# Attention scores on one core: waits folded into TensorE's matmuls, and one signal per tile from SyncE

## The chip, the cores and the metric

The kernel runs on one core of a Trainium2 chip. The metric is device microseconds of one execution, as the median of several runs; lower is better.

## The reference

```python
def setup_inputs():
    batch, heads, seq, dim = 8, 8, 512, 64
    # q, k: [8, 8, 512, 64] float32, normal

def reference(q, k):
    scale = 1.0 / np.sqrt(q.shape[-1])
    return (np.einsum('bhqd,bhkd->bhqk', q, k) * scale).astype(np.float32)
```

For each of 64 pairs of batch and head the 512 queries are multiplied with the 512 keys over a depth of 64, and scaled by 1/8. The inputs are 2 x 8.4 MB, the output is 67.1 MB of float32.

## The kernel before

**Tiles.** The batch is cut into four units (UNITS) of two batch entries. A unit's k and q are loaded in two DMAs of 2 MB into one of three buffers `big`, cast to bf16 by GpSimd into `xb`, turned by TensorE (`turn`, eight transposes with an identity into the PSUM tile `tp`) and moved by ScalarE and VectorE (`move`) into `kT` (keys) and `qz` (queries, with zeros so that two heads share one matmul of depth 128). A unit gives four output tiles of 4 MB (CHUNKS), so there are 16 tiles g = 0 to 15. A tile is one store DMA from a buffer `big`; the three buffers rotate, so tile g uses the buffer of tile g-3, and those of the loads before that.

**One tile.** `scores` makes eight pairs p = 0 to 7 of two matmuls (128 x 512 each) into the PSUM tiles `ps` p mod 3. The even pairs are scaled and copied to `big` by ScalarE, the odd ones by VectorE (`evacuator`, 128 x 1024 elements at once). Between pairs 2 and 3, as long as there is a later unit to prepare (g < 12), TensorE turns one chunk of it out of `xs`, which GpSimd has filled from `xb` (`fill`), and ScalarE and VectorE move it after their pairs 1 and 2.

**Order.** Nothing is scheduled by a planner: each engine has its own program, and semaphores order them. TensorE's tiles are a hardware loop (`pe.Fori`), so its semaphores are counted down again each time; `take` (L161) waits for a count and subtracts it in one instruction of TensorE's sequencer. The semaphores around the change are:

- `next`: tile g+1 may begin. SyncE raises it at L97, when ScalarE (`out_act`) and VectorE (`out_dve`) are done with their halves of tile g, and then issues the store of tile g (L98).
- `room`: the store buffer of the tile is free. For the first three tiles GpSimd raises it after the casts that read the buffer (L143); for the others it waits at L152 for the landing of store g-2 (`store_sems`) and raises it. TensorE takes it between the two matmuls of pair 0 (L171).
- `free0`, `free1`, `free2`: a PSUM tile is empty. Raised by the evacuation (L234), taken ahead of pairs 2 to 7.
- `ready`: `xs` is filled. `moved`: the turned chunk is in place. `turn`: a chunk is turned. `pe_act`, `pe_dve`: a pair is computed. `cast`: the buffer of the second unit has been read, so that the last unit can be loaded into it.

GpSimd does in one loop (L148) the fill for tile g's successor and then the wait for a landed store. SyncE's queue holds, in order, the six first loads, the two loads of the last unit (each behind `cast`), and the sixteen stores; at its end it waits for the last landings.

Of the kernel before, what the change touches and what calls it, by code (L numbers as in the profile page):

```python
# [5 lines left out]
def kernel(  # L6
# [5 lines left out]
    nc = tc.nc  # L12
# [3 lines left out]
    UNITS = B // 2  # L16
# [11 lines left out]
    CHUNKS = 4  # L28
    SLOTS = 12
    PAIRS = RO  # L30
# [4 lines left out]


    names = ["ready", "room", "moved", "zeroed", "ident", "turn", "pe_act", "pe_dve",
             "next", "free0", "free1", "free2", "out_act", "out_dve", "cast"]
    sem = {name: nc.alloc_semaphore(name) for name in names}
    load_sems = [nc.alloc_semaphore(f"load{n}") for n in range(2 * UNITS)]  # L40
    store_sems = [nc.alloc_semaphore(f"store{n}") for n in range(3)]
# [9 lines left out]
    qz = nc.alloc_sbuf_tensor("qz", [P, 2 * N, RO, P], bf16)[:]  # L51
    identity = nc.alloc_sbuf_tensor("identity", [P, P], f32)[:]
    tp = nc.alloc_psum_tensor("tp", [P, W, P], f32)[:]
    pss = [nc.alloc_psum_tensor(f"ps{n}", [P, 2, S], f32)[:] for n in range(3)]

    def words(ap):
        return ap.bitcast(f32)
# [7 lines left out]
    xsw = words(xs.rearrange("p w s d e -> p w (s d e)"))  # L65
    keys = kT.rearrange("p n m s j -> p n (m s j)")

    pe = nc.tensor
# [3 lines left out]
    def xf(v):  # L72
        return bigs[(0, 1, 2, 1)[v]].rearrange("p x i k -> p (x i k)").rearrange(
            "p (x s c) -> p x s c", x=2, s=2)

    def store_buffer(g):
        return bigs[(0, 2, 1)[g % 3]]

    def load(v, x):
        nc.sync.dma_start(out=xf(v)[:, x],  # L80
                          in_=(k_r, q_r)[x][v].rearrange("p (s c) -> p s c", s=2)
                          ).then_inc(load_sems[2 * v + x], 16)
# [6 lines left out]
    tc.compile()  # L89


    for x in range(2):
        nc.sync.wait_ge(sem["cast"], x + 1)
        load(UNITS - 1, x)
    for g in range(CHUNKS * UNITS):
        nc.sync.wait_ge(sem["out_act"], g + 1)
        nc.sync.wait_ge(sem["out_dve"], g + 1).then_inc(sem["next"], 1)  # L97
        nc.sync.dma_start(out=out_r[g], in_=store_buffer(g).rearrange("p x i k -> p x (i k)")  # L98
                          ).then_inc(store_sems[g % 3], 16)
    for n in range(3):  # L100
        nc.sync.wait_ge(store_sems[n], 16 * len(range(n, 4 * UNITS, 3)))

# [4 lines left out]
                            fill=1.0, base=0, pattern=[[-1, P]], channel_multiplier=1  # L107
                            ).then_inc(sem["ident"], 1)

    def fill(copy, c):  # L110
        w0 = c % SLOTS * W
        copy(out=xs.rearrange("p w s d e -> p (w s d e)"),  # L112
             in_=xb[:, w0:w0 + W].rearrange("p w s d e -> p (w s d e)")).then_inc(sem["ready"], 1)
# [11 lines left out]
    for v in range(UNITS):  # L125
        for x in range(2):
# [18 lines left out]
                nc.gpsimd.drain().then_inc(sem["cast"], 1)  # L145
            elif v == 1 and x == 1:
                last.then_inc(sem["cast"], 1)
    for g in range(2, CHUNKS * UNITS - 1):  # L148
        if g + CHUNKS < CHUNKS * UNITS:
            nc.gpsimd.wait_ge(sem["turn"], g + CHUNKS)  # L150
            fill(nc.gpsimd.tensor_copy, g + CHUNKS)
        nc.gpsimd.wait_ge(store_sems[(g - 2) % 3], 16 * ((g - 2) // 3 + 1)  # L152
                          ).then_inc(sem["room"], 1)


    def turn(src, dst):
        for w in range(W):
            ins = pe.transpose(out=dst[:, w], identity=identity, in_=src[:, w])  # L158
        ins.then_inc(sem["turn"], 1)

    def take(name, count=1):  # L161
        pe.wait_ge(sem[name], count).then_inc(sem[name], -count)  # L162


    def scores(n2, p):
        x, i = p // 4, p % 4 * 2
        if p != 1:
            take(f"free{p % 3}" if p else "next")
        ps = pss[p % 3]
        for w in range(2):  # L170
            if p == 0 and w == 1:  # L171
                take("room")
            ins = pe.matmul(out=ps[:, w, :],  # L173
                            lhsT=qz[:, bass.ds(n2 + x, 1), i + w].rearrange("p n c -> p (n c)"),
                            rhs=keys[:, bass.ds(n2 + x, 1)].rearrange("p n c -> p (n c)"),
                            start=True, stop=True)
        ins.then_inc(sem["pe_dve" if p % 2 else "pe_act"], 1)

    pe.wait_ge(sem["ident"], 2)
    first = [tp] + [ps.rearrange("p w (c k) -> p (w c) k", k=P) for ps in pss]  # L180
    for c in range(CHUNKS):
        take("ready")
        turn(xw[:, c * W:(c + 1) * W], first[c])
    take("moved", 4 * CHUNKS)
    for name in ("next", "free2"):
        pe.sem_inc(sem[name], 1)
    with pe.Fori(0, CHUNKS * UNITS) as g:
        n2 = g % (2 * TILES) * 2
        for p in range(3):
            scores(n2, p)  # L190
        with pe.If(g < CHUNKS * (UNITS - 1)):
            take("ready")
            turn(xsw, tp)
        for p in range(3, PAIRS):
            scores(n2, p)
        with pe.If(g < CHUNKS * (UNITS - 1)):
            take("moved", CHUNKS)
# [3 lines left out]
    def move(copy, c, s, tile_):  # L201
        v, t = divmod(c, CHUNKS)
        n0 = v % 2 * N
        h0 = t % 2 * W
        if t < 2:
            src = tile_[half(s)].rearrange("d j (n h m) -> d h n m j", n=N, h=2)
        else:
            src = tile_[half(s)].rearrange("d (i jj) (n h m) -> d h i n m jj", jj=JJ, n=N, h=2)
            h0 = t % 2 * IW
        for h in range(2):  # L210
            if t < 2:
                dst = kw[half(h), n0:n0 + N, :, s, h0:h0 + W]
            else:
                dst = qw[half(h), n0:n0 + N, h0:h0 + IW, h * U // 2:(h + 1) * U // 2].rearrange(
                    "d n i (m s jj) -> d s i n m jj", s=2, jj=JJ)[:, s]
            copy(out=dst, in_=src[:, h]).then_inc(sem["moved"], 1)  # L216

    def evacuator(engine, copy, scaled, parity, done, drained):
        if parity:
            for v in range(2):  # L220
                engine.memset(qz[:, v * N:(v + 1) * N], 0.0).then_inc(sem["zeroed"], 1)  # L221
        for c in range(CHUNKS):
            engine.wait_ge(sem["turn"], c + 1)
            if c == 2:
                engine.wait_ge(sem["zeroed"], 2)
            move(copy, c, parity, first[c])
        count = 0
        for g in range(CHUNKS * UNITS):
            o = store_buffer(g)
            for p in range(parity, PAIRS, 2):  # L230
                x, i = p // 4, p % 4 * 2
                count += 1
                engine.wait_ge(done, count)
                scaled(o[:, x, i:i + 2, :], pss[p % 3]).then_inc(  # L234
                    sem[f"free{p % 3}"] if p < PAIRS - 2 else drained, 1)
                c = g + CHUNKS
                if p in (1, 2) and c < CHUNKS * UNITS:
                    engine.wait_ge(sem["turn"], c + 1)
                    move(copy, c, parity, tp)
            if g == 0 and not parity:  # L240
                fill(copy, CHUNKS + 1)

    evacuator(nc.scalar, nc.scalar.copy,
              lambda o, ps: nc.scalar.mul(out=o, in_=ps, mul=scale),  # L244
              0, sem["pe_act"], sem["out_act"])
    evacuator(nc.vector, nc.vector.tensor_copy,
              lambda o, ps: nc.vector.tensor_scalar(out=o, in0=ps, scalar1=scale, scalar2=None,  # L247
                                                    op0=mult),
              1, sem["pe_dve"], sem["out_dve"])


# [28 lines left out]
```

## Time and profile before

| What | Value |
|---|---|
| Median of 4 runs | 202.82 us (202.73 to 202.82) |
| The profiled execution | 202.93 us, span 201.6 us |
| Mean granted TensorE clock | 0.797 |
| TensorE matmuls, busy | 102.9 us (51%) |
| VectorE, ScalarE, GpSimd, busy | 106.2, 87.2, 58.4 us |
| DMA | 83.91 MB, mean 416 GB/s |
| HBM read and written | 16.78 and 67.11 MB |

The span runs from the first to the last instruction; what lies around it belongs to the time too. In rows of the profile PE is the matmul side of TensorE, PEld its weight loads, PEq its sequencer, DVE is VectorE, ACT ScalarE, POOL GpSimd, and SPq the queue of SyncE, from which all DMAs are issued. What stands in brackets is the idle time ahead of an instruction and what ended it.

### The profile page before, as it was taken

Reading aid. Unit: us, or ns where it says so; the run is one execution under the profiler, and the core shown is the slowest. Engines: PE = TensorE matmul, PEld = TensorE weight load, DVE = VectorE, ACT = ScalarE, POOL = GpSimd, SP = SyncE. Lnnn points to the kernel's source line nnn. Section 1 sums busy time; section 2 is a strip of 40 time slices with the busy share of each in tenths; the row PEclk is TensorE's granted clock in tenths of the full one; section 3 lists DMA queues with packets and bytes.
Section 4 is the critical chain, followed back from the end, with each engine's and each line's share of the span. In section 5 each row is a group of like instructions: output and inputs, shape, how many; then the busy total and the mean of one; then the engine's idle time right before and its main releaser. Section 6 shows DMA issues by size and latency. Waiting matters only on the chain. (4 is left out here: it accounts for less than half of the span.)

```text
span 201.6 us, 1633 instructions
## 1 busy us (share of the span) xinstructions
PE 102.9 (51%) x384; PEld 48.7 (24%) x384; DVE 106.2 (53%) x98; ACT 87.2 (43%) x98; POOL 58.4 (29%) x34
## 2 busy tenths in 40 slices
PE   0027372365666649393936666654767575740000
PEld 0026140141424315051513233331212121210000
DVE  0666465084857694847478484759272636350000
ACT  0205575264646655464647464656344444440000
POOL 0399999999303030303030303030000000000000
PEclk9999979597878996969699797999585858585555
DMA  6999999999999999999999999999999999999993
GB/s 189 432 426 436 432 429 426 429 403 432 436 423 436 439 419 432 436 423 432 429 436 426 436 439 423 432 432 426 426 436 436 423 436 436 423 428 419 442 426 133
DMA packets 5507, 83.91 MB, mean 416 GB/s; under 512 B 384, under 2 KB 384, under 8 KB 384
## 3 DMA queue, kind: packets, MB, share of 16 engines
q1 hardware_dynamic: 5504, 83.89, 98.0%
q14 instruction: 3, 0.02, 0.0%
HBM read 16.78 MB, written 67.11 MB: 416 GB/s over the span
## 5 line engine op out<-in xcount | busy, mean ns | idle before, releaser
L173 PE MATMUL ps<-kT,qz 128*128 x256 | 84.3, 469 | 60.5 <-PEq L162 60.4
L247 DVE TENSOR_SCALAR big<-ps 128x1024 f32<-128x1024 f32 x64 | 77.1, 1222 | 53.6 <-PE ps L173 53.2
L244 ACT ACTIVATE big<-ps 128x1024 f32<-128x1024 f32 x64 | 65.2, 1024 | 72.2 <-PE ps L173 71.6
L173 PEld LDWEIGHTS ps<-kT,qz 128*128 x256 | 27.8, 108 | 108.8 <-issue 101.4
L112 POOL COPY xs<-xb 128x2048 bf16<-128x2048 bf16 x10 | 18.9, 1893 | 67.5 <-DMA out_dram<-big 67.3
L123 POOL CAST xb<-big 128x2048 bf16<-128x2048 f32 (+1 forms) x16 | 36.2, 2326 | 3.5 <-DMA big<-in_k_dram 3.0
L158 PEld LDWEIGHTS tp<-identity,xs 128*128 128x128 f32 x96 | 16.3, 188 | 5.4 <-issue 5.0
L158 PE MATMUL tp<-identity,xs 128*128 128x128 f32 x96 | 17.2, 340 | 0.4 <-PEq L162 0.4
L216 DVE COPY kT<-tp 64x512 f32<-64x512 f32 x14 | 9.7, 694 | 5.7 <-PE tp L158 5.3
L216 ACT COPY kT<-tp 64x512 f32<-64x512 f32 x14 | 8.1, 577 | 10.3 <-PE tp L158 10.0
L216 DVE COPY qz<-tp 64x512 f32<-64x512 f32 x12 | 8.3, 694 | 6.4 <-PE tp L158 6.2
L221 DVE MEMSET qz<- 128x4096 uint32 x2 | 6.9, 3472 | 6.7 <-PEq L89 5.9
L158 PE MATMUL tp<-identity,xb 128*128 128x128 f32 x8 | 1.9, 424 | 13.7 <-PEq L162 13.7
L216 ACT COPY qz<-tp 64x512 f32<-64x512 f32 x12 | 7.4, 621 | 2.8 <-PE tp L158 2.6
L158 PEld LDWEIGHTS tp<-identity,xb 128*128 128x128 f32 x8 | 1.6, 223 | 13.7 <-issue 13.7
L158 PE MATMUL ps<-identity,xb 128*128 128x128 f32 x24 | 3.9, 323 | 1.3 <-PEq L162 1.3
L158 PEld LDWEIGHTS ps<-identity,xb 128*128 128x128 f32 x24 | 3.5, 170 | 1.7 <-issue 1.7
L216 ACT ACT_TABLE_LOAD x1 | 1.3, 1283 | 5.0 <-PEq L89 5.0
L216 DVE COPY qz<-ps 64x512 f32<-64x512 f32 x4 | 2.8, 694 | 1.0 <-PE ps L158 0.9
L216 ACT COPY qz<-ps 64x512 f32<-64x512 f32 x4 | 2.5, 625 | 1.2 <-PE ps L158 1.2
L123 POOL CAST xs<-big 128x1024 bf16<-128x1024 f32 x2 | 2.7, 1333 | 0.2 <-DMA big<-in_k_dram 0.2
L112 ACT COPY xs<-xb 128x2048 bf16<-128x2048 bf16 x1 | 1.9, 1891 | 0.0
(8 smaller groups left out, 3.4 us busy)
## 6 DMA issues: line engine op xcount, KB each, us to landing
out_dram<-big SPq DMA_DIRECT2D x16, 4096.0 KB, 19.6
big<-in_k_dram SPq DMA_DIRECT2D x4, 2048.0 KB, 15.4
big<-in_q_dram SPq DMA_DIRECT2D x4, 2048.0 KB, 17.8
```

Of the source, the lines that this page charges most:

```text
L112: copy(out=xs.rearrange("p w s d e -> p (w s d e)"), in_=xb[:, w0:w0 + W].rearrange("p w s d e -> p (w s d e)")).then_inc(sem["ready"], 1)
L123: return nc.gpsimd.tensor_copy(out=dst, in_=src)
L158: ins = pe.transpose(out=dst[:, w], identity=identity, in_=src[:, w])
L173: ins = pe.matmul(out=ps[:, w, :], lhsT=qz[:, bass.ds(n2 + x, 1), i + w].rearrange("p n c -> p (n c)"), rhs=keys[:, bass.ds(n2 + x, 1)].re ...
L216: copy(out=dst, in_=src[:, h]).then_inc(sem["moved"], 1)
L221: engine.memset(qz[:, v * N:(v + 1) * N], 0.0).then_inc(sem["zeroed"], 1)
L244: lambda o, ps: nc.scalar.mul(out=o, in_=ps, mul=scale),
L247: lambda o, ps: nc.vector.tensor_scalar(out=o, in0=ps, scalar1=scale, scalar2=None, op0=mult),
```

## The change

TensorE no longer takes `next`, `free` and `ready` with an instruction that waits and subtracts. It waits with `wait_ge` ahead of the first matmul of a pair, and that matmul subtracts at its end. As the subtraction comes later now, neighbouring uses of one PSUM tile have semaphores of their own (`free0a`, `free0b` and so on, listed in `before` and `after` by pair). `room` is no longer taken by TensorE: SyncE issues the store of tile g, waits until the buffer of tile g+1 is free (`room` for the first tiles, else the landing of store g-2), and then raises `next`. GpSimd keeps only the fills. `out_act` and `out_dve` become one semaphore `out` that counts two per tile.

```diff
@@ names
-             "next", "free0", "free1", "free2", "out_act", "out_dve", "cast"]
+             "next", "free0a", "free0b", "free1a", "free1b", "free2a", "free2b",
+             "out", "cast"]
@@ SyncE
+    nc.sync.wait_ge(sem["room"], 1)
+    nc.sync.sem_inc(sem["next"], 1)
     for x in range(2):
         nc.sync.wait_ge(sem["cast"], x + 1)
         load(UNITS - 1, x)
+    def landed(g):
+        nc.sync.wait_ge(store_sems[g % 3], 16 * (g // 3 + 1))
+
     for g in range(CHUNKS * UNITS):
-        nc.sync.wait_ge(sem["out_act"], g + 1)
-        nc.sync.wait_ge(sem["out_dve"], g + 1).then_inc(sem["next"], 1)
+        nc.sync.wait_ge(sem["out"], 2 * g + 2)
         nc.sync.dma_start(out=out_r[g], in_=store_buffer(g).rearrange("p x i k -> p x (i k)")
                           ).then_inc(store_sems[g % 3], 16)
+        if g < CHUNKS * UNITS - 1:
+            if g >= 2:
+                landed(g - 2)
+            else:
+                nc.sync.wait_ge(sem["room"], g + 2)
+            nc.sync.sem_inc(sem["next"], 1)
@@ GpSimd
-    for g in range(2, CHUNKS * UNITS - 1):
-        if g + CHUNKS < CHUNKS * UNITS:
-            nc.gpsimd.wait_ge(sem["turn"], g + CHUNKS)
-            fill(nc.gpsimd.tensor_copy, g + CHUNKS)
-        nc.gpsimd.wait_ge(store_sems[(g - 2) % 3], 16 * ((g - 2) // 3 + 1)
-                          ).then_inc(sem["room"], 1)
+    for c in range(CHUNKS + 2, CHUNKS * UNITS):
+        nc.gpsimd.wait_ge(sem["turn"], c)
+        fill(nc.gpsimd.tensor_copy, c)
@@ TensorE
     def turn(src, dst):
         for w in range(W):
             ins = pe.transpose(out=dst[:, w], identity=identity, in_=src[:, w])
+            if w == 0 and dst is tp and src is xsw:
+                ins.then_inc(sem["ready"], -1)
         ins.then_inc(sem["turn"], 1)
+    before = ["next", None, "free2a", "free0a", "free1a", "free2b", "free0b", "free1b"]
+    after = ["free0a", "free1a", "free2b", "free0b", "free1b", "free2a", "out", "out"]
     def scores(n2, p):
-        x, i = p // 4, p % 4 * 2
-        if p != 1:
-            take(f"free{p % 3}" if p else "next")
-        ps = pss[p % 3]
         for w in range(2):
-            if p == 0 and w == 1:
-                take("room")
-            ins = pe.matmul(out=ps[:, w, :], ...
+            if w == 0 and before[p]:
+                pe.wait_ge(sem[before[p]], 1)
+            ins = pe.matmul(out=pss[p % 3][:, w, :], lhsT=weights(n2, p, w),
+                            ...
+            if w == 0 and before[p]:
+                ins.then_inc(sem[before[p]], -1)
         ins.then_inc(sem["pe_dve" if p % 2 else "pe_act"], 1)
@@ TensorE, ahead of the loop and in it
-    for name in ("next", "free2"):
-        pe.sem_inc(sem[name], 1)
+    pe.sem_inc(sem["free2a"], 1)
...
-            take("ready")
+            pe.wait_ge(sem["ready"], 1)
             turn(xsw, tp)
@@ evacuator
-                scaled(o[:, x, i:i + 2, :], pss[p % 3]).then_inc(
-                    sem[f"free{p % 3}"] if p < PAIRS - 2 else drained, 1)
+                scaled(o[:, x, i:i + 2, :], pss[p % 3]).then_inc(sem[after[p]], 1)
```

More of the change, by code (lines that the diff above doesn't have):

```diff
@@ L162, in take, with weights @@
         pe.wait_ge(sem[name], count).then_inc(sem[name], -count)
+    before = ["next", None, "free2a", "free0a", "free1a", "free2b", "free0b", "free1b"]
+    after = ["free0a", "free1a", "free2b", "free0b", "free1b", "free2a", "out", "out"]
+    def weights(n2, p, w):
+        return qz[:, bass.ds(n2 + p // 4, 1), p % 4 * 2 + w].rearrange("p n c -> p (n c)")
     def scores(n2, p):
-        x, i = p // 4, p % 4 * 2
-        if p != 1:
-            take(f"free{p % 3}" if p else "next")
-        ps = pss[p % 3]
         for w in range(2):
-            if p == 0 and w == 1:
-                take("room")
-            ins = pe.matmul(out=ps[:, w, :],
-                            lhsT=qz[:, bass.ds(n2 + x, 1), i + w].rearrange("p n c -> p (n c)"),
-                            rhs=keys[:, bass.ds(n2 + x, 1)].rearrange("p n c -> p (n c)"),
+            if w == 0 and before[p]:
+                pe.wait_ge(sem[before[p]], 1)
+            ins = pe.matmul(out=pss[p % 3][:, w, :], lhsT=weights(n2, p, w),
+                            rhs=keys[:, bass.ds(n2 + p // 4, 1)].rearrange("p n c -> p (n c)"),
                             start=True, stop=True)
+            if w == 0 and before[p]:
+                ins.then_inc(sem[before[p]], -1)
         ins.then_inc(sem["pe_dve" if p % 2 else "pe_act"], 1)
@@ L216, in move, with evacuator @@
             copy(out=dst, in_=src[:, h]).then_inc(sem["moved"], 1)
-    def evacuator(engine, copy, scaled, parity, done, drained):
+    def evacuator(engine, copy, scaled, parity, done):
         if parity:
@@ L244 @@
               lambda o, ps: nc.scalar.mul(out=o, in_=ps, mul=scale),
-              0, sem["pe_act"], sem["out_act"])
+              0, sem["pe_act"])
     evacuator(nc.vector, nc.vector.tensor_copy,
@@ L248 @@
                                                     op0=mult),
-              1, sem["pe_dve"], sem["out_dve"])
+              1, sem["pe_dve"])
 _INS = ['q', 'k']
```

## The prediction

> **What bounds the kernel now.** I read the page's parts from the second to the sixth, then short stretches at the end, then the order of time around one hand-over. In the page's slices the row that matters is DMA:
>
> ```profile
> DMA  6999999999999999999999999999999999999993
> ...
> q1 hardware_dynamic: 5504, 83.89, 98.0%
> ...
> PE 2%; DVE 1%; issue 0%
> ...
> out_dram<-big SPq DMA_DIRECT2D x16, 4096.0 KB, 19.6
> ```
>
> The sixteen DMA engines are full from the second slice to the last but one, and 98.0% of the span is packets of the one queue q1. The chain that ended last holds 3% of engine work; the rest is stores draining. A store lands 19.6 us after its issue, but the landings are 9.72 us apart (the first landing of store 2 is at 71.64 us, that of store 9 at 139.68 us in the trace's semaphore records: 68.04 / 7). So a store typically waits some 9 us in the queue: it is issued long before the DMA engines can take it. TensorE, the vector and the scalar engine are busy 51%, 53% and 43%.
>
> The floor of the DMA engines can be read from the packets. Each engine moves 320 packets of 16 KB; most of them take 611 ns, whatever runs beside them. 320 x 0.611 = 195.5 us after a first packet at 1.96 us is 197.5 us. The end looks so (stretch, its length, busy times by engine, clock, DMA share, GB/s):
>
> ```profile
> 195.00:197.90 2.90, 0.00 (x0) 0.00 (x0) 0.00 (x0) 0.00 (x0) 0.00 (x0) 0.50 1.03 441
> 197.90:198.50 0.60, 0.00 (x0) 0.00 (x0) 0.00 (x0) 0.00 (x0) 0.00 (x0) 0.50 0.14 55
> 198.50:201.20 2.70, 0.00 (x0) 0.00 (x0) 0.00 (x0) 0.00 (x0) 0.00 (x0) 0.50 0.06 24
> ```
>
> The reader is to see the share of 0.06 in the last 2.70 us: that is 1/16, one DMA engine alone. Fifteen are done by 198.5, the sixteenth at 201.14, and its landing at 201.57 ends the span of 201.6. The profiled execution took 202.93 us, so 1.33 us lie around the span; the median of the runs is 0.11 us lower.
>
> This sixteenth engine does not fall behind at once. From store 2 to store 9 the last landings go from 72.72 to 142.58 us, 9.98 us apart, so it loses 0.26 us a store; in the last three stores, with the other engines silent, it loses nothing more (3.50, 3.37 and 3.23 us behind the first one). Its packets take 625 to 650 ns where TensorE's instructions are dense and about 611 to 620 ns where they are sparse. From 44 to 148 us the trace holds 1053 instructions and 529 semaphore updates, 148 in 9.72 us. If the loss goes with them, each record costs this engine 0.25 / 148 = 1.7 ns. This is a correlation in one trace; a common cause may be behind both.
>
> **The hand-over, part by part.** This is one boundary between tiles and one wait inside a tile (start, length, engine, line):
>
> ```profile
> 65.01 0.22 PEld L173 LDWEIGHTS ps<-kT,qz 128*128 x2 [2.20 <-issue]
> ...
> 66.09 1.22 DVE L247 TENSOR_SCALAR big<-ps 128x1024 f32<-128x1024 f32 x1 [0.23 <-PE ps L173]
> 67.41 0.37 SPq L98 DMA_DIRECT2D out_dram<-big  x1
> ...
> 67.82 1.53 PE L173 MATMUL ps<-kT,qz 128*128 x6 [1.77 <-PEq L162]
> ...
> 72.87 1.89 POOL L112 COPY xs<-xb 128x2048 bf16<-128x2048 bf16 x1 [8.09 <-DMA out_dram<-big]
> ```
>
> and this the view of the line of take (engine, operation, count: shortest, median and longest ns):
>
> ```profile
> L162 PEldq EVENT_SEMAPHORE  x157: 51/51/51, 13.6 to 177.9; - x157
> ```
>
> Removed: eight of these 51 ns sequencer instructions per tile (next, room, six free). In the built program the waits sit on the register instructions (ISA) of the following matmul and the decrements on the matmul itself, so they do leave; ready keeps its own instruction and loses only its decrement. One step, from the start of such an instruction to that of the next, takes 0.15 us where the wait has just ended (64.764 to 64.915). On a tile's path I count three: next, room between the first two matmuls, and the blocking wait ahead of the seventh pair, 3 x 0.15 = 0.45 us. The other five stand under evacuations and transposes; without that cover they are worth up to 0.75 us more a tile.
>
> Added on that path: SyncE gives next after the store's issue, not before. The issue takes 0.37 us (0.33 to 0.61 over all 24), the event that follows 0.03 us plus some 0.05 us of dispatch, which is how SyncE's own rows follow each other (67.340 event, 67.414 issue). Sum 0.45 us. So the tile's time is about unchanged; my ends are -0.3 (the waits elsewhere count as well) and +0.8 us (the slowest issue, 0.61, plus 0.2 of dispatch, and nothing saved). I take 0, as the 0.37 us row is the median of this very instruction. Tile 1 pays once more: now its first matmul ran at 33.65 and only the second waited for room until 38.65; after, both start then, about 0.5 us later.
>
> The Trainium skill has a rule that speaks against the change: "TensorE: Matmul & The Clock Gate", section "The cost: per-tile semaphore tail", has semaphore updates of matmuls serialise at 26.3 ns each, so eight decrements would be 0.21 us more a tile as an estimate. The rows here have no matmul with two updates, so no run shows it. It would leave the end where it is, for the reason that follows.
>
> Moved: the wait for store g-2 goes from GpSimd, where it stood ahead of the next fill (67.3 us idle in the page, 8.09 us before the fill at 72.87), to SyncE behind the issue of store g. On SyncE only the next store's issue is queued behind it, and that store's tile cannot start without the same signal, so nothing that is ready is held up. The fills of 1.89 us may now run earlier, which nothing on the path waits for. At the start SyncE waits for room (the casts of the first unit end at 18.5 us) ahead of the two last loads; the first of these is issued at 23.86 anyway, on cast. The issue order of all 24 DMAs is the same. out_act and out_dve become one count of two per tile, at the same place.
>
> **Why this hardly moves the end.** The DMA engines run dry only if a store is issued too late. From issue to the first landing of the store before I find 4.7, 4.4 and 4.2 us for stores 1, 2, 3 (store 3: issue 67.41, first landing of store 2 at 71.64), 5.7 to 6.0 for 4 to 7, 7.2 to 8.8 for 8 to 15. An issue takes 1.0 us to its first packet (0.95 to 1.96 at the start), so 3.2 us are free at the narrowest. With 0 per hand-over and 0.5 once, 2.7 us remain. From tile 12 on (store 9 lands 142.58, tile 11's store is issued at 141.23) the tile starts on a landing and not on the hand-over, so nothing adds up there.
>
> What is left is the one slow DMA engine. A tile has 8 fewer instructions on TensorE, 13/16 fewer on GpSimd (the 13 room events) and 29/16 fewer updates of room: 10.6 records. 10.6 x 1.7 ns = 18 ns, over the twelve stores in which the loss grows 0.22 us. Ends: zero, if those records do not count, and 0.75 us, if each costs the 4.7 ns steps in which the packet times differ (10.6 x 4.7 ns x 15). I take 0.22, the mean of its own rows. 202.93 - 0.22 = 202.71 profiled, less 0.11 is 202.6 us as median.
>
> The skill has such an engine too: "DMA: Bandwidth & Descriptors", section "Latency and other measured facts", finds two of the engines usually slower, and guesses that software-made descriptor rings do it, which queues of SyncE do not use. The trace differs: only hardware_dynamic packets run here, and one engine is 3.2 us late. By that rule the change would move the end by 0 and the time would be 202.82.
>
> **The rivals.** About 0.2% (0.4 us) is what a measurement of this kernel can tell from no change.
>
> 1. The forecast: the DMA engines stay full, the tail of one engine shrinks by 0 to 0.4 us. 202.42 to 202.82, with the runs' scatter of 0.1. For it: 98.0%, the free 3.2 us. Chance 0.76; a fetch of code that lands on the slow engine instead (three such packets of 309 ns are in the span, none on it) gives 203.1 and counts with the slower.
>
> 2. Faster: the slow engine's loss is made mostly by TensorE's sequencer and hand-overs, so that removing eight of them per tile takes 0.4 to 0.75 us. 202.07 to 202.4. For it: its packet times follow TensorE's instructions. Against: matmuls and weight loads, which stay, follow them at least as well. A faster tile alone cannot give this, since no DMA engine waits for a tile now. Chance 0.17.
>
> 3. Slower: next given later makes the tile the bound. Tiles 1 to 11 are set by their own length (stores 67.41, 75.62, 85.15, 94.98: 8.2 to 9.9 us a tile against 9.72 us of DMA), so a dearer hand-over adds up from tile to tile. It decides from (7.2 - 1.0) / 10 = 0.62 us more per hand-over, at store 10. At my end of 0.8 us the DMA engines stand 8.0 - 6.2 = 1.8 us and the time is 204.6 us. A lower TensorE clock (0.8 to 1.0 in these stages) would do the same. Against: it needs both the slowest issue and no saving. Chance with the code fetch 0.07.
>
> **The numbers.** Same 0.76, faster 0.17, slower 0.07. The range from 202.25 to 202.95 leaves out the far half of rival 2 and nearly all of rival 3, under 2 in 10.
>
> **What would show it.** Right: DMA share 98%, the same first and last landings within 0.5 us, 17 events left on the line of take and 12 on that of ready (157 on L162 before), next one issue later, store 3 issued within 68.5 us, and a last engine 2.8 to 3.2 us behind the others. Wrong: a slice of DMA under 9 between the second and the last, a store issued after the first landing of the store before it (rival 3), or a last engine less than 2.8 us late (rival 2).

## The result, and the profile after

The changed kernel takes 202.48 us (median of 40 runs, 202.33 to 202.80) against 202.78 us before (60 runs, 202.65 to 203.14). The ratio is 0.9986, with a 95% interval of 0.9982 to 0.9991: 0.30 us less, clear of the scatter and within the 0.2% that the prediction called no change.

The same parts of the page of the changed kernel (slices of DMA, queue q1, chain), in the page's order:

```profile
DMA  5999999999999999999999999999999999999993
...
q1 hardware_dynamic: 5504, 83.89, 98.1%
...
DMA 34%; PE 21%; DVE 15%; POOL 10%; POOLq 4%; issue 3%; SPq 1%
```

The DMA engines are as full as before. The chain now reads quite differently (34% DMA, 21% TensorE instead of 3% in all), although the limit is the same: SyncE now waits for a landing, and TensorE's matmuls name SyncE as what released them, so that the trace can be followed back through the stores. It takes both: with either part of the change alone (below) the chain stays at 2 or 3%. The chain is a path of releases and no list of what costs time.

The end, as stretches of the changed kernel (stretch, length, busy times by engine, clock, DMA share, GB/s):

```profile
195.00:197.90 2.90, 0.00 (x0) 0.00 (x0) 0.00 (x0) 0.00 (x0) 0.00 (x0) 0.50 1.03 441
197.90:198.50 0.60, 0.00 (x0) 0.00 (x0) 0.00 (x0) 0.00 (x0) 0.00 (x0) 0.50 0.08 27
198.50:201.20 2.70, 0.00 (x0) 0.00 (x0) 0.00 (x0) 0.00 (x0) 0.00 (x0) 0.50 0.04 18
```

One engine is still alone at the end, but it has less to do: a share of 0.04 over the last 2.70 us against 0.06 before. In the semaphore records the last landing of the last store is 2.83 us behind its first one; before it was 3.23. This distance is called the arrears of the last engine below. The first landing itself moved from 198.34 to 198.27 us, the fifteenth from 199.29 to 198.81. So 0.40 us of the 0.48 us by which the last landing moved (201.57 to 201.09) lie in this one engine's arrears.

The hand-over of the same tile, in the order of time:

```profile
64.02 1.03 PE L186 MATMUL ps<-kT,qz 128*128 x4 [1.36 <-DVE big L259]
...
66.34 0.37 SPq L103 DMA_DIRECT2D out_dram<-big  x1
...
67.08 1.62 PE L186 MATMUL ps<-kT,qz 128*128 x6 [2.03 <-SPq L110]
```

TensorE now waits for VectorE and for SyncE's event at L110 directly, where the rows of before named its own sequencer (PEq L162). Of the 157 events on the line of take 17 are left, and 12 plain waits for ready:

```profile
L172 PEldq EVENT_SEMAPHORE  x17: 51/51/51, 13.6 to 139.9; - x17
...
L205 PEldq EVENT_SEMAPHORE  x12: 51/51/51, 24.2 to 133.4; - x12
```

### The profile page after: what moved, and what is told of

Same layout as the page of the kernel before. It is cut to its first block, busy times and chain, and to the rows that moved or that the text cites. A ratio compares the mean times of both kernels' runs of the same rounds, so it can differ in the third digit from the quotient of the medians.

```text
span 201.1 us, 1491 instructions
## 1 busy us (share of the span) xinstructions
PE 101.9 (51%) x384; PEld 51.0 (25%) x384; DVE 106.1 (53%) x98; ACT 87.0 (43%) x98; POOL 58.3 (29%) x34
## 4 chain that ended last, share of the span: by engine, by line
DMA 34%; PE 21%; DVE 15%; POOL 10%; POOLq 4%; issue 3%; SPq 1%
DMA out_dram<-big 31%; PE ps L186 16%; DVE big L259 11%; POOL xb L134 9%; PE tp L166 5%; DMA big<-in_k_dram 4%; POOLq L154 4%; DVE kT L229 3%; DVE qz L229 1%; POOL xs L134 1%; SPq L103 1%; POOLq L156 1%; SPq L110 0%; SPq L90 0%; SPq L85 0%
## 5 line engine op out<-in xcount | busy, mean ns | idle before, releaser
L186 PE MATMUL ps<-kT,qz 128*128 x256 | 81.4, 466 | 61.4 <-SPq L110 42.5
L186 PEld LDWEIGHTS ps<-kT,qz 128*128 x256 | 28.4, 111 | 107.3 <-issue 97.8
L166 PE MATMUL tp<-identity,xs 128*128 128x128 f32 x96 | 19.6, 374 | 0.0
L166 PEld LDWEIGHTS tp<-identity,xs 128*128 128x128 f32 x96 | 17.9, 202 | 4.4 <-issue 3.7
```

The costliest lines, as they stand in the source:

```text
L186: ins = pe.matmul(out=pss[p % 3][:, w, :], lhsT=weights(n2, p, w), rhs=keys[:, bass.ds(n2 + p // 4, 1)].rearrange("p n c -> p (n c)"), sta ...
```

## The experiments

Two readings of the 0.30 us stand against each other. *Records*: each instruction and semaphore update of the engines costs the sixteenth DMA engine a little, and the change has 142 instructions fewer (1633 to 1491 in the trace). *Hand-overs*: the tiles or their signals became cheaper. A third one says that this engine's path is simply slow.

| Kernel | Time, us | Ratio to before | Instructions, updates in the trace | Last landing of the last store behind the first, us |
|---|---|---|---|---|
| before | 202.78 | | 1633, 1228 | 3.23 |
| changed | 202.48 | 0.9986 (0.9982 to 0.9991) | 1491, 1198 | 2.83 |
| DMAs alone | 200.16 | 0.9868 (0.9852 to 0.9883) | 76, 683 | 0.58 |
| TensorE's part | 202.62 | 0.9988 (0.9979 to 0.9997) | 1505, 1229 | 2.93 |
| SyncE's part | 202.78 | 1.0000 (0.9990 to 1.0009) | 1603, 1204 | 1.73 |
| 16 events on TensorE | 203.54 | 1.0046 (1.0023 to 1.0070) | 1731, 1454 | 0.98 |
| 24 increments behind next | 205.36 | 1.0122 (1.0104 to 1.0140) | 1851, 1565 | 5.59 |
| 24 drains behind next | 205.02 | 1.0109 (1.0091 to 1.0127) | 1851, 1205 | 5.31 |
| 24 increments ahead of next | 217.45 | 1.0719 (1.0692 to 1.0747) | 1851, 1566 | 0.79 |
| changed, loop written out | 202.06 | 0.9958 (0.9944 to 0.9972) | 1234, 1205 | 2.51 |
| before, loop written out | 202.05 | 0.9958 (0.9945 to 0.9972) | 1257, 1238 | 2.35 |
| no preparation | 201.73 | 0.9947 (0.9933 to 0.9960) | 1184, 1104 | 2.02 |

The instructions are those that the trace holds. It lacks 16 matmuls each in TensorE's part, SyncE's part and the 16 events on TensorE, and 7 in the kernel before with its loop written out.

**The DMAs alone.**

```diff
+    for g in range(CHUNKS * UNITS):
+        ...   # g < 3: wait for the loads of the buffer
+        if g >= 2:
+            nc.sync.wait_ge(store_sems[(g - 2) % 3], 16 * ((g - 2) // 3 + 1))
+        nc.sync.dma_start(out=out_r[g], in_=store_buffer(g)...).then_inc(store_sems[g % 3], 16)
-    (all work of TensorE, VectorE, ScalarE and GpSimd)
```

> Leaves out all computing: SyncE issues the same eight loads and sixteen stores in the same order and paced by the landing of store g-2; what is stored is what was loaded. Theory (records): the sixteenth DMA engine falls behind because the instructions and semaphore updates of the engines cost it time. With hardly any of them its last landing of the last store is at most 0.9 us behind the first one (2.83 us in the changed kernel, 3.23 before), and the time is 202.48 - 2.0 = 200.5 us or a little less. Rival (the engine's own path is slow): it is 2.8 us or more behind here too, 202.4 us. Rival (hand-overs): the same, 202.4 us.

Measured: 200.16 us; the last landing is 0.82 us behind the first in store 0, 0.87 to 0.89 in stores 3 to 11 and 0.58 at the end. The end of this kernel as stretches (stretch, length, GpSimd busy, clock, DMA share, GB/s):

```profile
195.00:197.90 2.90, 0.00 (x0) 1.00 0.95 407
197.90:198.50 0.60, 0.00 (x0) 1.00 0.01 0
198.50:201.20 2.70, 0.00 (x0) 1.00 0.00 0
```

No engine is left alone after 198.5. With idle compute engines the same stores at the same pace (first landings 52.2 to 198.2 us, as before) keep all sixteen together. The single packets say the same: from 50 to 140 us all 2372 of this kernel take 611 ns, while 137 of 2366 in the changed kernel take longer (625 ns in the median), about the share of one engine (148). So the arrears are not a property of that engine's path; they come with the work of the other engines. That rules out the third reading. It does not yet say which work: with the instructions, what the engines read and write is gone here too. No kernel here with these DMAs in this order was faster, so some 2.3 us (202.48 - 200.16) are the most that this order leaves above it.

**The two parts of the change, each alone on the kernel before.** The first keeps room, GpSimd's waits and next ahead of the issue, the second keeps take:

```diff
  TensorE's part
-            take(f"free{p % 3}" if p else "next")
+            pe.wait_ge(sem[before[p]], 1) ... ins.then_inc(sem[before[p]], -1)
  SyncE's part
-        nc.sync.wait_ge(sem["out_dve"], g + 1).then_inc(sem["next"], 1)
+        nc.sync.wait_ge(sem["out_dve"], g + 1)
         nc.sync.dma_start(...)
+        ...   # wait until the buffer of tile g+1 is free
+        nc.sync.sem_inc(sem["next"], 1)
-        nc.gpsimd.wait_ge(store_sems[(g - 2) % 3], ...).then_inc(sem["room"], 1)
-            if p == 0 and w == 1:
-                take("room")
```

> Only TensorE's part of the change on the kernel before (next, free and ready waited for ahead of a matmul and subtracted by it, semaphores doubled, out counted together); room, its waits on GpSimd and next ahead of the store's issue stay as before. Theory (records): 7 instructions fewer a tile, 7 x 1.7 ns x 12 = 0.14 us faster than before at the price used in the prediction, 0.2 us if instructions of TensorE's sequencer cost more: 202.55 to 202.65 us. Rival (hand-overs): all of the gain, 202.48 us. Rival (room on GpSimd and TensorE is what counted): 202.78 us.

> Only SyncE's part on the kernel before: next after the issue of the store and after the buffer is free, no room on TensorE, no waits for stores on GpSimd; TensorE keeps its waiting and subtracting instructions. Theory (records): one instruction fewer on TensorE, 0.8 on GpSimd and 1.8 updates a tile, 3.6 x 1.7 ns x 12 = 0.07 us faster than before: 202.7 us. Rival (a later next makes the tile the bound): slower than before, over 203 us. Rival (the wait moved off GpSimd made the gain): 202.48 us.

Measured: 202.62 us for TensorE's part, where records said 202.55 to 202.65, and 202.78 us for SyncE's, where they said 202.7 (the interval of 0.9990 to 1.0009 holds it). TensorE's part is the one that gains; its interval also holds the whole gain, 202.48 us. It has 112 instructions fewer (128 in the trace, less the 16 missing matmuls) and 0.30 us less of arrears, 2.7 ns each; by the time, 0.16 us, it would be 1.4 ns. What SyncE's part alone did was not expected: its stores 3 to 11 are issued 10.24 us apart (67.4, 77.6, ... 149.3), more than the 9.72 us of DMA, and the first landing of the last store came at 199.62 us, 1.28 us later than before. The DMA engines did run dry, as rival 3 has it (stretches, columns as above):

```profile
148.00:149.00 1.00, 0.00 (x0) 0.00 (x0) 1.00 (x1) 0.54 (x1) 0.00 (x0) 1.00 0.69 295
149.00:150.00 1.00, 0.00 (x0) 0.00 (x0) 0.18 (x1) 0.00 (x0) 0.00 (x0) 1.00 0.67 279
150.00:151.00 1.00, 0.85 (x3) 0.38 (x4) 0.00 (x0) 0.00 (x0) 0.00 (x0) 0.54 1.23 524
```

Two stretches stand at 0.69 and 0.67 ahead of one at 1.23 (a packet is counted where it starts). But the time stayed: the fast engines stood while the slow one used the pause to catch up, from 2.32 to 1.73 us behind. In this run a dry queue cost nothing, being shorter than the arrears of the last engine.

**More events on TensorE.**

```diff
             take("moved", CHUNKS)
+        for n in range(16):
+            pe.sem_inc(sem["extra"], 1 - n % 2 * 2)
```

> The changed kernel with sixteen semaphore events added per tile on TensorE, behind the last matmul of the tile, where TensorE waits some 2 us for the evacuations anyway. Theory (records): 32 records more a tile (16 instructions, 16 updates) x 1.7 ns = 54 ns, over twelve stores 0.65 us: 203.1 us, last landing 3.4 to 3.6 us behind the first. Rival (the gain came from cheaper hand-overs or shorter tiles): the events stand beside other work, 202.5 us and 2.8 us.

Measured: 203.54 us, in the direction of the records, but not a clean test: the last landing was 0.98 us behind the first and not 3.4 to 3.6. Until store 5, while nothing was late, the last landing falls back 0.27 us a store (0.89, 1.16, 1.43, 1.71) against 0.22 in the changed kernel (0.87, 1.07, 1.33, 1.54). Then the longer tiles (stores 10.2 us apart from store 3 to 11) ran the queue dry, and the first landing of the last store came at 200.92. The two costs cannot be parted here.

**More records where nothing waits.** SyncE is idle behind its signal for the next tile:

```diff
             nc.sync.sem_inc(sem["next"], 1)
+            for n in range(24):
+                nc.sync.sem_inc(sem["extra"], 1)     # second kernel: nc.sync.drain()
```

> The changed kernel with 24 semaphore increments per tile added on SyncE, behind its signal for the next tile (360 instructions and 360 updates). Nothing waits for them and SyncE is idle there for 8 us. From the runs so far: between the kernel with the DMAs alone and the kernel before lie 2.64 us and 2102 records (instructions and semaphore updates), 1.26 ns each. Theory (records of any engine): 720 x 1.26 ns = 0.9 us, 203.4 us, the last landing 3.6 us or more behind the first. Rival (only TensorE's instructions): 202.5 us and 2.8 us.

> The same place with 24 drains of SyncE instead, which touch no semaphore: 360 instructions, no updates. Theory (instructions and updates count alike): 0.45 us, 202.9 us. If updates alone count: 202.5 us. If instructions alone count: as much as with the increments, 203.4 us.

Measured: 205.36 and 205.02 us. That is far from the 202.5 us of the rival, and the first landings stand where they stood (198.3 at the last store): all of it is the sixteenth engine, 5.59 and 5.31 us behind. The end of the kernel with the drains, in stretches (columns as above):

```profile
198.50:201.20 2.70, 0.00 (x0) 0.00 (x0) 0.00 (x0) 0.00 (x0) 0.00 (x0) 0.50 0.06 24
201.20:204.00 2.80, 0.00 (x0) 0.00 (x0) 0.00 (x0) 0.00 (x0) 0.00 (x0) 0.50 0.04 18
```

It is alone for more than 5 us. But the expected sizes were far too small, for two reasons. About half of the rise is steady: between stores 2 and 5 it falls back 0.33 us a store with the increments and 0.31 with the drains, against 0.22 in the changed kernel. The other half comes in three steps, at stores 2, 6 and 11 (0.65, 0.77, 0.81 us with the increments, the steady part included). At these times the trace has packets of code (62.7, 109.8 and 158.0 us; 8 KB, 309 to 318 ns each), which neither the kernel before nor the changed one has there. They are SyncE's: they come after 99, 229 and 359 of its instructions here, and after as many in the kernel of the next experiment, where that is at 66.7, 123.2 and 178.4 us. And they go through the engine that ends last: the packet that each of them follows took 629 to 661 ns, and before 140 us only one engine's packets are so long. Without some 0.45 us for each of the three the drains leave (5.31 - 2.83 - 1.35) / 360 = 3 ns an instruction, and the increments 4 ns for an instruction and an update together. That splitting is an estimate from two kernels. The drains read and write no data, so instructions alone are enough to raise the arrears.

**A later signal.** The 24 increments ahead of next:

```diff
+            for n in range(24):
+                nc.sync.sem_inc(sem["extra"], 1)
             nc.sync.sem_inc(sem["next"], 1)
```

> The 24 increments ahead of the signal for the next tile, so that every hand-over is later by about 24 x 0.06 = 1.5 us. Rival 3 of the prediction with a price above its point: tiles 1 to 11 pile up 15 us against 5 to 7 us that were free, the DMA engines run dry for some 8 us. Theory (the engine that ends last has 2.5 us of arrears and takes no part in the first 2.5 us of that): 202.5 + 0.9 + 8 - 2.5 = 209 us, the last landing of the last store less than 1 us behind the first. Rival (hand-overs are still hidden): 203.4 us.

Measured: 217.45 us. The page's slices show the queue run dry again and again, and q1's share fall:

```profile
DMA  6999999999999598969699998969897999999997
...
q1 hardware_dynamic: 5504, 83.89, 92.1%
```

Rival 3's mechanism is real above its point, and the last engine was never more than 1.03 us behind, as the theory said. The size was missed by more than half: 6.5 us over the changed kernel were worked out and 15.0 came. Stores 1 to 11 are 11.43 us apart against 9.34 in the changed kernel, 2.09 us more and not 1.5. 24 events at the 58 ns by which they follow each other are 1.4 us. The other 0.7 us go with the clock: the changed kernel has three tiles of 8.3 us at a granted TensorE clock of 1.00 among others of 9.1 to 11.0 us at 0.81 to 0.84, and here all ten stand at 0.71 to 0.85. Why the clock was lower is left open.

**The loop written out,** for both kernels:

```diff
-    with pe.Fori(0, CHUNKS * UNITS) as g:
+    for g in range(CHUNKS * UNITS):
```

> The changed kernel with TensorE's loop over the tiles written out: no address instructions, no branches, some 370 records fewer; the matmuls, their waits and their order stay. Theory (records): 370 x 1.26 ns = 0.47 us, 202.0 us, last landing 2.2 to 2.5 us behind the first; the longer program may bring five more code packets of 309 ns, up to 1.5 us if all fell to the engine that ends last. Rival (only what changes hand-overs counts): 202.5 us.

> The kernel before with TensorE's loop written out, to be set beside the changed kernel with the loop written out (202.06 us). There the wait of the changed kernel has no address instruction to ride on and is an instruction of its own again (145 such on TensorE, 162 in this one), so that only 17 instructions on TensorE, 13 on GpSimd and some 30 updates stand between the two. Theory (records, at the 2.5 to 3.5 ns an instruction and 0.7 ns an update that the drains and increments on SyncE showed between code packets): 0.1 us, 202.15 us. Rival (the change gains by its hand-overs): 0.3 us as in the loop, 202.35 us or more.

Measured: 202.06 and 202.05 us. Written out, a matmul has no address instruction ahead of it on which a wait could ride, so the waits of the changed kernel are 51 ns events of their own again:

```profile
L185 PEldq EVENT_SEMAPHORE  x112: 51/51/51, 22.9 to 177.3; - x112
```

So the first kernel drops 369 address and branch instructions of TensorE and gets 112 events, 257 instructions fewer (1491 to 1234) and not the 370 records of the expectation. It beats both kernels of this case: 0.42 us, where 0.47 was expected, and 0.31 us less of arrears. That is 1.2 to 1.6 ns an instruction, for instructions that are no hand-over. The second, set beside the first, is the same pair as before and after, with only 30 instructions between the two (23 in the traces, one of which lacks 7 matmuls), and no gain of the change is seen any more (0.1 expected by the records, 0.3 by the hand-overs; the arrears are 0.16 us larger in the first). With intervals of 0.28 us to either side this leans to the records and does not settle it; and as the waits are events in both kernels, TensorE's hand-overs hardly differ here either. What speaks for the count of instructions is that it moves the arrears where no hand-over changes: in the drains above, and below.

**No preparation.**

```diff
-            turn(xsw, tp)
...
-                    move(copy, c, parity, tp)
...
-        fill(nc.gpsimd.tensor_copy, c)
```

> The changed kernel without the preparation of the later units: no transposes, moves and fills in tiles 0 to 11 (all tiles use the first unit's scores); loads and casts stay. That is some 290 instructions and 100 updates fewer, none of them in the hand-over of tiles. Theory (records, at 2.5 to 3.5 ns and 0.7 ns): 0.8 to 1.1 us less, 201.4 to 201.7 us, the last landing 1.8 to 2.1 us behind the first. At the mean of 1.26 ns: 202.0 us. Rival (tiles that end sooner bring nothing and records cost nothing): 202.5 us.

Measured: 201.73 us, 2.02 us behind; in the time just above what the records said, in the arrears within it. 307 instructions fewer than in the changed kernel take 0.81 us of arrears, 2.6 ns each if all is put on them. What is left out here is no hand-over of tiles. (The data of the moves and fills are gone too.)

## Why the prediction was right

*The limit.* Sixteen full DMA engines, floor at 198.5 us, one engine alone to the end: as read, but that fifteen are done by 198.5 us holds for fourteen (the fifteenth landed at 199.29). The time moved only as far as the last engine did. Two of the signs held by little: that engine was 2.83 us behind, and under 2.8 was to speak for rival 2; its last landing moved by 0.48 us of the 0.5 allowed.

*The tile.* The prediction had 0.45 us added and 0.45 us saved. In the trace, from the end of VectorE's last evacuation to the first matmul of the next tile it is 0.76 us (66.316 to 67.080) against 0.51 (67.313 to 67.820): 0.26 us later, where 0.45 less 0.15 was worked out. The blocking wait ahead of the seventh pair costs 0.14 us (63.878 to 64.019) against 0.29: 0.15 saved, as worked out. Only room was priced too high: the two matmuls of pair 0 start 0.22 us apart instead of 0.28, so 0.06 was saved and not 0.15. Stores 1 to 11 are 9.34 us apart on average, before 9.38. Tile 1 came 0.85 us later and not 0.5 (issue 48.33 against 47.48), and the narrowest margin is 3.9 us (first landing of store 0 at 52.23) where 4.2 was.

*The size.* 0.22 us was forecast and 0.30 measured in the time, with an interval of 0.18 to 0.36 that holds the forecast. In the arrears it is 0.40, but the traced execution of before was 0.15 us above the median of its kernel, so the time is the better measure. The term that seems too small is the price of a record. 1.7 ns was the mean over all instructions and updates; the change takes out mostly instructions, and these cost 2.6 to 3 ns in two experiments (no preparation, drains), an update under 1 (0.28 us for 360). The slope agrees: from store 2 to 9 the last landings are now 9.954 us apart and the first ones 9.730, a loss of 0.22 us a store against 0.26, so 36 ns less and not 18. But in the loop written out an instruction cost 1.2 to 1.6 ns. The price is thus no single number, and that the forecast came so near is in part luck.

*Rival 2* was thus nearer than its chance in kind, but not in reach: 0.3 us and not over 0.4. *Rival 3* was priced wrongly in its first two microseconds. It would not have begun to cost at 0.62 us a hand-over, where the queue first runs dry, but only when it stands for longer than the last engine's arrears, as SyncE's part alone showed with 1.28 us of delay and no loss. Beyond that it cost more than was worked out (24 increments ahead of next: 15.0 us and not 6.5).

*The two rules of the Trainium skill.* "TensorE: Matmul & The Clock Gate", section "The cost: per-tile semaphore tail", has 26.3 ns for each increment when every one of many small packed matmuls makes one. In the changed kernel a matmul that subtracts is followed by the next after 225 ns (64.019 to 64.244), and before, without subtraction, after 224 (65.017 to 65.241): no cost is seen here, where updates come a whole matmul apart. "DMA: Bandwidth & Descriptors", section "Latency and other measured facts", guesses that two engines are slower because of software-made descriptor rings. Only hardware_dynamic packets carried data here and one engine was slower all the same; it fell behind less with fewer instructions, and not at all when the compute engines were idle.

## What to carry to other kernels

Where stores fill the DMA engines from end to end, look at the last landing of each store beside the first, and not at the mean share: the end belongs to one engine, and it can be moved although everything else is hidden. Then instructions count a little, also where nothing waits for them (here on TensorE and SyncE), and a hand-over is worth about what it drops in instructions; a wait that rides on an instruction that is there anyway saves, one that needs its own does not. Judge a longer hand-over by the margin of the queue and the arrears of the last engine together.

## What the runs showed of the hardware

- One DMA engine of sixteen loses some 1 to 3 ns for each instruction that the core's engines run while stores flow: 3 ns for each of SyncE's drains, which touch no semaphore and no data, 1.2 to 1.6 ns for the address and branch instructions of TensorE's loop. ScalarE and VectorE were not tried alone, and whether what they read and write adds to it stays open. Every execution here was taken with the profiler on, so it stays open whether the instructions cost this or the recording of them.
- The code packets of SyncE (8 KB) go through that same engine, some 0.45 us for each by estimate. Code packets at other times (78.6 us in the changed kernel) left its arrears alone.
- With the loop of TensorE written out the last landing of store 1 was 1.94 us behind the first at once, and the arrears stayed near that until store 7, so another engine was probably last till then. A code packet of 16 KB (961 ns, at 55.5 us) comes just before; two more (91.1 and 139.8 us) were not followed further.
